# A gate matrix stored by group of 96 tokens, and one-hot tiles with the row number innermost, in a two-layer decoder trunk

## The chip, the core and the metric

The kernel runs on one core of one Trainium2 chip. The core has five engines that work through their own instruction lists in order: TensorE (PE, with its weight loads listed apart as PEld), VectorE (DVE), ScalarE (ACT), GpSimd (POOL) and SyncE (SP). ACT, SP and POOL also issue DMA transfers, and 16 DMA engines carry them out. The metric is the device time of one execution in microseconds (us), lower is better.

## What is computed

The reference is a decoder trunk of two layers on 512 tokens of width 1024. Each layer has a mixer (a gated linear recurrence and a state-space branch), which the change does not touch, and then a PEER block: 8 heads choose 16 of 16384 single-neuron experts for each token.

```python
s1_v, s1_i = lax.top_k(s[:, :, 0, :], PEER_TOPK)
s2_v, s2_i = lax.top_k(s[:, :, 1, :], PEER_TOPK)
cand_v = (s1_v[..., :, None] + s2_v[..., None, :])...
top_v, top_j = lax.top_k(cand_v, PEER_TOPK)
idx = jnp.take_along_axis(cand_i, top_j, axis=-1)
gate = jax.nn.softmax(top_v, axis=-1)
act = jax.nn.gelu(einsum('thkd,td->thk', u_tab[idx], hb))
out = einsum('thk,thkd->td', gate * act, v_tab[idx])
```

An expert number is 128 times a first index plus a second index, so the 16384 experts are a square of 128 by 128.

## The kernel before

For the first 384 tokens (TD) the kernel does not gather. It computes the activation of all 16384 experts and multiplies it by a gate matrix that is zero wherever an expert was not chosen. For the last 128 tokens it gathers the chosen rows. A layer's PEER block has these parts:

- **Scores and select.** `select(tb)` finds, for a block of 128 tokens, the 128 chosen expert numbers of each token and their gates. Most of it is DVE work, among it 128 small operations that write the tile `jk` (L875).
- **Build.** `build(tb, sel, g8)` makes the gate matrix for 4 tokens. There are 96 builds in a layer. For each token it needs a one-hot matrix of the first indices (`P_`, L920), one of the second indices (`Q_`, tile `Qo`, L922) and the second one times the gate, split into two f16 parts (`Q`, L926, twice). A tile has 128 slots (partitions), 128 row numbers and 4 tokens, 512 f16 elements in a partition. DVE makes all four tiles by TENSOR_TENSOR, comparing `io4`, which holds the row numbers, with the token's slot numbers, which are broadcast along the row numbers. PE multiplies `P_` by the two `Q` tiles for each token (L932 and L933, 8 matmuls of 128x128 in a build, into PSUM tile `pa`, two buffers), and ACT copies the result to `stg` (L934). `stg` has one buffer and holds 96 tokens (SG), 24 builds. When it is full, ACT's queue issues four DMAs (L938), each for 32 of the 128 first indices, to the DRAM matrix `sW`. `sW` is ordered by first index, second index, token, with 384 tokens in a row.
- **U matmuls.** `dense_U` multiplies 128 blocks of the expert table by the activations. A block is loaded (`raw`, 512 KB, issued by SP), split by ACT into `whi` (L113) and by DVE into `wlo` (L115), goes through 24 matmuls on PE (L131 to L133, PSUM tile `mm`, three buffers), then through a GELU on ACT into `uo` (L797, two buffers) and to DRAM (`sA`, L798).
- **Gather steps.** `gather_steps` fetches 128 rows of the U table and then 128 rows of the V table, each 512 KB, with DMAs that POOL issues; DVE does a product with each U row (L967) and adds each V row to `gacc` (L978).
- **V matmuls.** For each of the 128 first indices, `gated` loads one row block of `sA` and one of `sW` (tiles `A` and `W`, issued by SP), multiplies them on DVE (L1023), splits the product (`gh` on ACT, `gl` on DVE), and `vmm` does 24 matmuls (L1036 to L1038). The accumulators take all PSUM banks, and a gate block is complete only when all four groups of 96 tokens are in DRAM, so no V matmul starts before the last group has landed.

The code writes builds, U matmuls and gather steps side by side. A list scheduler puts the instructions in each engine's order when the program is built. In layer 0 the work of preparing layer 1's state-space branch (`next_layer`) is added to the V part; in layer 1 it is not.

In this document the **build stage** is the stretch from a layer's first `P_` to the last copy into `stg`, the **gap** is from there to the first V matmul, and the **V stage** follows it.

Of the kernel before, what the change touches and what calls it, by code (L numbers as in the profile page):

```python
# [4 lines left out]
F32 = mybir.dt.float32  # L5
F32R = mybir.dt.float32r
F16 = mybir.dt.float16
# [4 lines left out]
OP = mybir.AluOpType  # L12
# [7 lines left out]
L = 2  # L20
# [7 lines left out]
HPN = 500  # L28
TD = 384
SG = 96  # L30
GB = 3
HALVES = (slice(0, T // 2), slice(T // 2, T))
EPS = 1e-6
# [7 lines left out]
def trunk(tc, a, dbg=None, layers=L, n_i2=128):  # L41
    nc = tc.nc
    V, S, G, TE = nc.vector, nc.scalar, nc.gpsimd, nc.tensor
    uid = [0]

    def nm(s):
        uid[0] += 1
        return f"{s}{uid[0]}"
# [3 lines left out]
    cst = ctx.enter_context(tc.tile_pool(name="cst", bufs=1))  # L52
# [3 lines left out]
    drp = ctx.enter_context(tc.tile_pool(name="drp", bufs=1, space=DRAM))  # L56
    PB = {"mm": 3, "pa": 2, "pb": 2, "pc": 1}

    def ptile(shape, tag):
        return psp.tile(shape, F32, tag=tag, name=nm(tag), bufs=PB[tag])  # L60
# [11 lines left out]
    it = ctmp.tile([128, 128], I32, name="it")  # L72
# [3 lines left out]
    V.memset(ones, 1.0)  # L76
    iof = cst.tile([128, 128], F32, name="iof")
    V.tensor_copy(iof, it)
    io4 = cst.tile([128, 128, 4], F16, name="io4")
    V.tensor_copy(io4, it[:, :, None].to_broadcast([128, 128, 4]))  # L80
    masks = cst.tile([128, 6, 128], U8, name="masks")
    xo = ctmp.tile([128, 128], I32, name="xo")
    V.tensor_tensor(xo, ip, it, op=OP.bitwise_xor)
# [705 lines left out]


    sA = [drp.tile([128, 128, TD], F32, name=f"sA{l}") for l in range(L)]
    sW = [drp.tile([128, 128, TD], F32, name=f"sW{l}") for l in range(L)]

    def dense_U(l, i, h, pool):
        ps = dense(a["u"][l, i], h, n=TD)
# [22 lines left out]
    def peer(l, h, rows, gp):  # L818
# [85 lines left out]
        stg = {}  # L904

        def build(tb, sel, g8):
            st, gh = sel
            NT = 4
            c = slice(NT * g8, NT * g8 + NT)
            t0 = 128 * tb + NT * g8  # L910
            n, o = divmod(t0, SG)
            if o == 0:
                stg[0] = rp.tile([128, 128, SG], F32, tag="stg", name=nm("stg"), bufs=1)
            sh = [128, 128, NT]

            def row(t):
                return t[:, None, :].to_broadcast(sh)

            P_ = rp.tile(sh, F16, tag="P", name=nm("P"))
            V.tensor_tensor(P_, io4, row(st[:, 0, c]), op=OP.is_equal)  # L920
            Q_ = rp.tile(sh, F16, tag="Qo", name=nm("Qo"))
            V.tensor_tensor(Q_, io4, row(st[:, 1, c]), op=OP.is_equal)  # L922
            Qs = []
            for i in range(2):
                q = rp.tile(sh, F16, tag=f"Q{i}", name=nm("Q"))
                V.tensor_tensor(q, Q_, row(gh[:, i, c]), op=OP.mult)  # L926
                Qs.append(q)
            for b in range(NT // 4):
                ps = ptile([128, 4, 128], "pa")
                for k in range(4):  # L930
                    t = 4 * b + k
                    TE.matmul(ps[:, k], P_[:, :, t], Qs[0][:, :, t], start=True, stop=False)  # L932
                    TE.matmul(ps[:, k], P_[:, :, t], Qs[1][:, :, t], start=False, stop=True)  # L933
                S.activation(stg[0][:, :, o + 4 * b:o + 4 * b + 4], ps[:].rearrange("p t i -> p i t"), AF.Copy,  # L934
                             scale=1.0 / GATE)
            if o + NT == SG:
                for q in range(0, 128, 32):
                    nc.scalar.dma_start(sW[l][q:q + 32, :, SG * n:SG * n + SG].rearrange("i p t -> p i t"),  # L938
                                        stg[0][:, q:q + 32])


        def gather_ids(fx):
# [12 lines left out]
        def gather(tab, ids, s_):  # L955
            g = gp.tile([128, D], F32, tag="gr", name=nm("gr"), bufs=GB)
            G.indirect_dma_start(out=g[:], out_offset=None, in_=tab,  # L957
                                 in_offset=bass.IndirectOffsetOnAxis(ap=ids[:, s_:s_ + 1], axis=0))
            return g
# [43 lines left out]
        for tb in range(NB - 1):  # L1003
            sel = select(tb)
            for g8 in range(32):
                build(tb, sel, g8)
                if g8 % 2:
                    more(1)
                    gsteps(1)
# [7 lines left out]
        vctx = ExitStack()  # L1017
        vp = vctx.enter_context(tc.tile_pool(name=f"vp{l}", bufs=2))

        def gated(i, A):  # L1020
            W = vp.tile([128, TD], F32, tag="W", name=nm("W"), bufs=3)
            nc.sync.dma_start(W, sW[l][i])
            V.tensor_tensor(A, A, W, op=OP.mult)  # L1023
            gh = vp.tile([128, TD], F32R, tag="gh", name=nm("gh"), bufs=4)
            S.activation(gh, A, AF.Copy)  # L1025
            gl = vp.tile([128, TD], F32R, tag="gl", name=nm("gl"), bufs=4)
            V.tensor_tensor(gl, A, gh[:].bitcast(F32), op=OP.subtract)  # L1027
            return gh, gl
# [19 lines left out]
        def spilled(i):  # L1048
            w = wv(i)
            A = vp.tile([128, TD], F32, tag="A", name=nm("A"), bufs=3)  # L1050
            nc.sync.dma_start(A, sA[l][i])
            return w, gated(i, A)
# [35 lines left out]
    for k in ("adab", "n1g", "n2g", "glub"):  # L1088
        sh = a[k].shape
# [12 lines left out]
    for j in range(J):  # L1102
        m = cst.tile([128, 2], F32, name=nm("m"))
        for k in range(2):
            t = ad0.tile([128, D], F32, tag="ada", name=nm("ada"))
# [35 lines left out]
    for l in range(layers):  # L1141
        h = norm_mod(gain1[l], shift1[l], ssq, G if l == 0 else None)
        mixer(l, h)
        dump(f"x1_{l}", xT)
        gain2 = mod_gain(l, 4, vec["n2g"][:, l, :])
        gp = tc.alloc_tile_pool(name=f"gp{l}", bufs=1, side="right")
        rows = gp.tile([128, D], F32, name=f"rows{l}")
        h2 = norm_mod_halves(col(gain2), col(mod[l], 24), rows)
        ssq = None

        ssq = peer(l, h2, rows, gp)
        gp.release()
        dump(f"x2_{l}", xT)
# [61 lines left out]
```

## Time and profile before

| | |
|---|---|
| time, median of 3 runs | 4118.07 us (4112.74 to 4119.02) |
| time of the profiled execution | 4119.27 us |
| its span (first to last instruction) | 4117.5 us |
| TensorE clock granted, mean over the span | 0.956 of full speed |
| PE / DVE / ACT / POOL busy | 3748.1 / 3272.4 / 1576.5 / 897.0 us |
| share of the chain that ended last: PE / DVE / DMA / ACT's queue | 67% / 14% / 7% / 4% |
| layer 0: build stage, gap, V stage | 930.6 to 1457.8, to 1497.0, to 2116 us |
| layer 1: build stage, gap, V stage | 2997.9 to 3523.3, to 3560.8, to 4093.5 us |

Busy time is the time in which an engine has at least one instruction under way; instructions that overlap are not counted twice. The chain that ended last is followed back from the end of the program, at each step to what released the instruction. "ACTq" is ACT's instruction queue, here while it issues DMAs. The rows that are read further down come in numbered groups.

### The profile page before, as it was taken

The numbers are of one execution on the slowest core, as the hardware profiler recorded it, in microseconds if no ns is written. First come the engines' busy times: TensorE is split into PE (matmuls) and PEld (weight loads), VectorE is DVE, ScalarE is ACT, GpSimd is POOL, SyncE is SP. The second block draws the span as 40 slices with busy tenths as digits, with TensorE's granted clock in tenths as the row PEclk, the third lists the DMA queues.
The fourth block names the chain that finished last, engine by engine and source line by source line (L and its number), as shares of the span: only waits on it lengthen the run. The fifth ranks groups of instructions, "written<-read, shape, count | busy, mean of one in ns | idle before, by whom it ended". The sixth has DMA issues, their size and how long they took to land.

```text
span 4117.5 us, 63112 instructions
## 1 busy us (share of the span) xinstructions
PE 3748.1 (91%) x21878; PEld 3506.5 (85%) x21878; DVE 3272.4 (79%) x9052; ACT 1576.5 (38%) x2510; POOL 897.0 (22%) x1139
## 2 busy tenths in 40 slices
PE   6999999999698856989999999999996988699998
PEld 5888878999597856889998888789996878699998
DVE  6998778999797769998757777779997976688874
ACT  3554534434233322344443445333342333233332
POOL 7443100033132235532000000000331213222210
PEclk9999999999798978999999999999998989899999
DMA  5222462498788899999843334624987788999994
GB/s 193 72 68 73 156 195 85 150 333 306 215 285 262 281 295 329 362 355 327 280 155 117 123 116 161 211 89 143 322 305 238 262 261 283 306 348 344 347 311 142
DMA packets 463889, 947.60 MB, mean 230 GB/s; under 512 B 169728, under 2 KB 288576, under 8 KB 461520
## 3 DMA queue, kind: packets, MB, share of 16 engines
q1 hardware_dynamic: 220448, 572.75, 41.0%
q0 software_dynamic: 73952, 268.56, 18.9%
q10 hardware_dynamic: 169168, 102.25, 8.4%
q8 instruction: 172, 2.82, 0.3%
q14 instruction: 149, 1.22, 0.1%
HBM read 814.44 MB, written 128.97 MB: 229 GB/s over the span
## 4 chain that ended last, share of the span: by engine, by line
PE 67%; DVE 14%; DMA 7%; ACTq 4%; issue 4%; ACT 2%; POOL 2%; SPq 0%; DVEq 0%; POOLq 0%
PE mm L131 11%; PE mm L132 11%; PE mm L133 11%; ACTq L938 3%; DVE jk L875 3%; PE mm L1037 3%; PE mm L1038 3%; PE mm L1036 3%; DVE wlo L115 3%; DMA gr<-ur,idi 2%; DMA gr<-v,idi 2%; PE pa L933 2%; PE pa L932 2%; PE pa L1037 2%; PE pb L1037 2%
## 5 line engine op out<-in xcount | busy, mean ns | idle before, releaser
L131 PE MATMUL mm<-ahi,whi 128*128 128x384 f32 (+1 forms) x3360 | 1225.2, 366 | 88.3 <-ACT uo L797 82.2
L113 ACT ACTIVATE whi<-raw 128x1024 fp32r<-128x1024 f32 x688 | 727.9, 1059 | 1350.6 <-PE mm L132 755.5
L132 PE MATMUL mm<-alo,whi 128*128 128x384 f32 (+1 forms) x3360 | 1221.6, 364 | 15.7 <-DVE alo L122 15.7
L133 PE MATMUL mm<-ahi,wlo 128*128 128x384 f32 (+1 forms) x3360 | 1221.5, 365 | 9.2 <-DVE wlo L115 9.0
L115 DVE TENSOR_TENSOR wlo<-raw,whi 128x1024 fp32r<-128x1024 f32 x688 | 840.9, 1223 | 378.8 <-ACT whi L113 377.8
L131 PEld LDWEIGHTS mm<-ahi,whi 128*128 128x128 f32 x3360 | 643.4, 192 | 141.1 <-ACT uo L797 86.0
L132 PEld LDWEIGHTS mm<-alo,whi 128*128 128x128 f32 x3360 | 642.4, 191 | 65.5 <-DVE alo L122 17.3
L133 PEld LDWEIGHTS mm<-ahi,wlo 128*128 128x128 f32 x3360 | 641.7, 191 | 62.4 <-DVE wlo L115 13.8
L957 POOL DMA_INDIRECT gr<-ur,idi x256 | 278.7, 1089 | 1498.4 <-DVE jk L875 567.4
L957 POOL DMA_INDIRECT gr<-v,idi x256 | 374.9, 1465 | 737.6 <-DVE gacc L978 645.0
L978 DVE SCALAR_TENSOR_TENSOR gacc<-gr,gate,gacc 128x1024 f32<-128x1024 f32 x254 | 324.6, 1278 | 38.1 <-DMA gr<-v,idi 38.0
L1036 PE MATMUL mm<-gh,whi 128*128 128x384 f32 x768 | 217.8, 341 | 141.4 <-ACT gh L1025 55.5
L967 DVE SCALAR_TENSOR_TENSOR gr<-gr,rows 128x1024 f32<-128x1024 f32 x256 | 311.1, 1217 | 17.6 <-DMA gr<-ur,idi 17.1
L1037 PE MATMUL mm<-gl,whi 128*128 128x384 f32 x768 | 260.8, 340 | 5.7 <-DVE gl L1027 5.3
L1036 PEld LDWEIGHTS mm<-gh,whi 128*128 128x128 f32 x768 | 141.8, 191 | 145.1 <-ACT gh L1025 97.7
L1038 PE MATMUL mm<-gh,wlo 128*128 128x384 f32 x768 | 254.2, 337 | 0.3 <-DVE wlo L115 0.3
L1025 ACT ACTIVATE gh<-A 128x384 fp32r<-128x384 f32 x256 | 132.7, 520 | 284.9 <-DVE A L1023 280.8
L932 PE MATMUL pa<-Q,P 128*128 128x128 f16 x768 | 197.3, 296 | 25.1 <-DVE P L920 15.9
L875 DVE SCALAR_TENSOR_TENSOR jk<-iof,tf,ci 128x50 f32<-128x50 f32 x1024 | 220.1, 267 | 0.0
L934 ACT ACTIVATE stg<-pa 128x512 f32<-128x512 f32 x192 | 114.2, 598 | 241.8 <-PE pa L933 239.5
L933 PE MATMUL pa<-Q,P 128*128 128x128 f16 x768 | 189.0, 296 | 0.2
L1036 PE MATMUL pb<-gh,whi 128*128 128x384 f32 x512 | 173.3, 338 | 0.0
(410 smaller groups left out, 6541.8 us busy)
## 6 DMA issues: line engine op xcount, KB each, us to landing
raw<-u SPq DMA_DIRECT2D x256, 512.0 KB, 5.1
raw<-v SPq DMA_DIRECT2D x256, 512.0 KB, 5.5
raw<-win SPq DMA_DIRECT2D x112, 512.0 KB, 3.7
ada<-ada SPq DMA_DIRECT2D x96, 512.0 KB, 4.8
sA<-uo ACTq DMA_DIRECT2D x256, 192.0 KB, 4.5
sW<-stg ACTq DMA_DIRECT2D x32, 1536.0 KB, 15.2
A<-sA SPq DMA_DIRECT2D x256, 192.0 KB, 5.2
W<-sW SPq DMA_DIRECT2D x256, 192.0 KB, 5.3
```

The source lines that it names most:

```text
L113: S.activation(hi, raw, AF.Copy)
L115: V.tensor_tensor(lo, raw, hi[:].bitcast(F32), op=OP.subtract)
L131: TE.matmul(ps, hi[:, w], ah, start=(j == 0), stop=False)
L132: TE.matmul(ps, hi[:, w], al, start=False, stop=False)
L133: TE.matmul(ps, lo[:, w], ah, start=False, stop=(j == J - 1))
L875: V.scalar_tensor_tensor(jk, iof[:, 0:NCAND], tf[:, hh, k:k + 1], ci[:, hh], op0=OP.is_equal, op1=OP.mult, accum_out=code[:, hh, k:k + 1])
L957: G.indirect_dma_start(out=g[:], out_offset=None, in_=tab, in_offset=bass.IndirectOffsetOnAxis(ap=ids[:, s_:s_ + 1], axis=0))
L967: V.scalar_tensor_tensor(g, g, 1.0, rows, op0=OP.mult, op1=OP.mult, accum_out=dot[:, s_:s_ + 1])
L978: V.scalar_tensor_tensor(acc_, g, gate[:, s_:s_ + 1], acc_, op0=OP.mult, op1=OP.add)
L1036: TE.matmul(ps, w[0][:, c], g[0], start=first, stop=False)
L1037: TE.matmul(ps, w[0][:, c], g[1], start=False, stop=False)
L1038: TE.matmul(ps, w[1][:, c], g[0], start=False, stop=last)
```

## The change

The gate matrix `sW` is now ordered by group of 96 tokens, second index, first index, token in the group. A partition of `stg` holds, for one second index, the first indices and their 96 tokens, so a store of 32 first indices writes 12288 contiguous bytes for a partition; before it wrote 32 pieces of 384 bytes. The loads of the V part now take two first indices at a time (WG), for all four groups: 512 pieces of 768 bytes, where two loads of 128 pieces of 1536 bytes stood. The tile `W` has two buffers of two blocks, before three of one.

The one-hot tiles turn from (row number, token) to (token, row number). `io4` and the four tiles lie in the new order; the slot and gate operands are now broadcast along the innermost dimension, so that in a run of 128 elements they give the same value again and again. Before, they were broadcast along the middle one, and their innermost run was the 4 tokens. PE reads a token's 128 columns from neighbouring places, before from every fourth.

```diff
+WG = 2
...
-    io4 = cst.tile([128, 128, 4], F16, name="io4")
-    V.tensor_copy(io4, it[:, :, None].to_broadcast([128, 128, 4]))
+    io4 = cst.tile([128, 4, 128], F16, name="io4")
+    V.tensor_copy(io4, it[:, None, :].to_broadcast([128, 4, 128]))
...
-    sW = [drp.tile([128, 128, TD], F32, name=f"sW{l}") for l in range(L)]
+    sW = [drp.tile([TD // SG, 128, 128, SG], F32, name=f"sW{l}") for l in range(L)]
...
-            sh = [128, 128, NT]
+            sh = [128, NT, 128]
...
-                return t[:, None, :].to_broadcast(sh)
+                return t[:, :, None].to_broadcast(sh)
...
-                    TE.matmul(ps[:, k], P_[:, :, t], Qs[0][:, :, t], start=True, stop=False)
-                    TE.matmul(ps[:, k], P_[:, :, t], Qs[1][:, :, t], start=False, stop=True)
+                    TE.matmul(ps[:, k], P_[:, t], Qs[0][:, t], start=True, stop=False)
+                    TE.matmul(ps[:, k], P_[:, t], Qs[1][:, t], start=False, stop=True)
...
-                    nc.scalar.dma_start(sW[l][q:q + 32, :, SG * n:SG * n + SG].rearrange("i p t -> p i t"),
-                                        stg[0][:, q:q + 32])
+                    nc.scalar.dma_start(sW[l][n, :, q:q + 32], stg[0][:, q:q + 32])
...
-            W = vp.tile([128, TD], F32, tag="W", name=nm("W"), bufs=3)
-            nc.sync.dma_start(W, sW[l][i])
-            V.tensor_tensor(A, A, W, op=OP.mult)
+            k = i % WG
+            if k == 0:
+                wt[0] = vp.tile([128, TD // SG, WG, SG], F32, tag="W", name=nm("W"), bufs=2)
+                nc.sync.dma_start(wt[0], sW[l][:, :, i:i + WG].rearrange("n p i t -> p n i t"))
+            Av = A[:].rearrange("p (n t) -> p n t", t=SG)
+            V.tensor_tensor(Av, Av, wt[0][:, :, k], op=OP.mult)
```

The scheduler puts the instructions in another order. Between a layer's first and 49th `P_`, DVE makes 50 `wlo` tiles before the change and 80 after it; between the first and last one, 20 additions to `gacc` before and 55 after it in layer 0 (18 and 54 in layer 1). The products with U rows (95) and the `jk` operations (250) in that stretch are as many as before.

The first place is DVE in layer 0 in the third group of 24 builds. Qo, P and Q are the one-hot tiles, gr and gacc belong to gather steps, wlo to a U matmul block. Before:

```order
L922 TENSOR_TENSOR Qo_11646<-io_83,slot_11420 128x512
L920 TENSOR_TENSOR P_11589<-io_83,slot_11420 128x512
L926 TENSOR_TENSOR Q_11593<-Qo_11591,gh_11422 128x512
L926 TENSOR_TENSOR Q_11595<-Qo_11591,gh_11422 128x512
L115 TENSOR_TENSOR wlo_14978<-raw_14974,whi_14976 128x1024
L920 TENSOR_TENSOR P_11644<-io_83,slot_11420 128x512
L967 SCALAR_TENSOR_TENSOR gr_15415,dot_8446<-gr_15415,rows_6308 128x1024
```

The same place on DVE after the change:

```order
L921 TENSOR_TENSOR P_11589<-io_83,slot_11420 128x512
L978 SCALAR_TENSOR_TENSOR gacc_6543<-gr_17504,gate_8444,gacc_6543 128x1024
L927 TENSOR_TENSOR Q_11575<-Qo_11573,gh_11422 128x512
L927 TENSOR_TENSOR Q_11577<-Qo_11573,gh_11422 128x512
L927 TENSOR_TENSOR Q_11593<-Qo_11591,gh_11422 128x512
L927 TENSOR_TENSOR Q_11595<-Qo_11591,gh_11422 128x512
L978 SCALAR_TENSOR_TENSOR gacc_6543<-gr_17546,gate_8444,gacc_6543 128x1024
```

The U blocks are gone from this stretch (they stand ahead of it now), and additions to `gacc` stand in the place of products with U rows.

The second place is ACT in layer 0 around the third store of `stg`; whi and uo belong to U blocks, dot to the gather steps. Before:

```order
L938 DMA sW_121<-stg_10488 128x32x96 x4
L970 ACTIVATE dot_8446<-dot_8446 128x32
L113 ACTIVATE whi_15124<-raw_15122 128x1024
L797 ACTIVATE uo_15042<-mm_15017 128x384
L798 DMA sA_119<-uo_15042 128x384
```

After the change:

```order
L935 ACTIVATE stg_10488<-pa_11670 128x128x4
L939 DMA sW_121<-stg_10488 128x3072 x4
L935 ACTIVATE stg_11721<-pa_11730 128x128x4
L935 ACTIVATE stg_11721<-pa_11748 128x128x4
L935 ACTIVATE stg_11721<-pa_11803 128x128x4
```

Behind the store stands at once the first copy into the next `stg`, which needs the buffer that the store is reading.

## Rows read from the trace of the kernel before

**Rows 1.** The page: the chain that ended last, by line.

```profile
PE mm L131 11%; PE mm L132 11%; PE mm L133 11%; ACTq L938 3%; DVE jk L875 3%; PE mm L1037 3%; PE mm L1038 3%; PE mm L1036 3%; DVE wlo L115 3%; DMA gr<-ur,idi 2%; DMA gr<-v,idi 2%; PE pa L933 2%; PE pa L932 2%; PE pa L1037 2%; PE pb L1037 2%
```

**Rows 2.** Stages: length, busy PE, PEld, DVE, ACT, POOL, clock, DMA share, GB/s.

```profile
930.60:1457.80 527.20, 455.73 (x2772) 431.32 (x2771) 423.52 (x1274) 177.52 (x270) 133.86 (x117) 0.92 0.83 266
1457.80:1497.00 39.20, 0.00 (x0) 0.00 (x0) 11.35 (x18) 4.11 (x6) 6.23 (x6) 0.50 1.00 268
1497.00:2116.00 619.00, 549.48 (x3071) 541.65 (x3071) 525.40 (x1139) 238.85 (x356) 193.59 (x116) 0.95 0.90 321
2997.90:3523.30 525.40, 454.95 (x2772) 431.48 (x2771) 422.38 (x1273) 178.44 (x271) 136.40 (x116) 0.92 0.83 267
3523.30:3560.80 37.50, 0.00 (x0) 0.00 (x0) 9.90 (x11) 3.50 (x5) 7.03 (x6) 0.50 1.02 284
3560.80:4093.50 532.70, 532.68 (x3071) 532.68 (x3071) 399.87 (x487) 196.63 (x254) 106.98 (x101) 1.00 0.89 314
```

**Rows 3.** ACT around the second store, in order of time: start, length, idle before.

```profile
1229.58 22.70 ACTq L938 DMA_DIRECT2D sW<-stg  x4
1252.38 1.06 ACT L113 ACTIVATE whi<-raw 128x1024 fp32r<-128x1024 f32 x1 [22.83 <-issue]
```

**Rows 4.** DVE's waits in layer 0's build stage: total us, times, longest.

```profile
DVE wlo L115 <- ACT whi L113: 59.9, 24, 23.1
DVE gate L971 <- ACT dot L970: 20.2, 1, 20.2
DVE P L920 <- PE pa L933: 10.5, 14, 1.5
DVE Q L926 <- PE pa L932: 8.3, 6, 3.2
```

**Rows 5.** DVE instructions by form over the run: busy us, mean ns, idle before.

```profile
L926 DVE TENSOR_TENSOR Q<-Qo,gh 128x512 f16<-128x512 f16 x384 | 149.2, 421 | 19.1 <-PE pa L932 19.0
L920 DVE TENSOR_TENSOR P<-io,slot 128x512 f16<-128x512 f16 x192 | 80.2, 420 | 21.6 <-PE pa L933 20.8
L922 DVE TENSOR_TENSOR Qo<-io,slot 128x512 f16<-128x512 f16 x192 | 78.1, 418 | 0.0
...
L757 DVE TENSOR_TENSOR ya<-ya,sg 128x512 f32<-128x512 f32 x16 | 11.0, 685 | 0.0
...
L115 DVE TENSOR_TENSOR wlo<-raw,whi 128x1024 fp32r<-128x1024 f32 x688 | 840.9, 1223 | 378.8 <-ACT whi L113 377.8
...
L978 DVE SCALAR_TENSOR_TENSOR gacc<-gr,gate,gacc 128x1024 f32<-128x1024 f32 x254 | 324.6, 1278 | 38.1 <-DMA gr<-v,idi 38.0
```

**Rows 6.** PE in order of time, f16 build matmuls and f32 U matmuls.

```profile
986.51 0.30 PE L933 MATMUL pa<-Q,P 128*128 128x128 f16 x1
986.63 0.30 PE L932 MATMUL pa<-Q,P 128*128 128x128 f16 x1
...
988.17 0.33 PE L131 MATMUL mm<-ahi,whi 128*128 128x384 f32 x1
...
988.52 0.33 PE L133 MATMUL mm<-ahi,wlo 128*128 128x384 f32 x1
```

**Rows 7.** DMA queues from 1230 to 1262 us (packets, MB, share of 16 engines).

```profile
q10 hardware_dynamic: 16645, 6.57, 80.2%
...
q1 hardware_dynamic: 288, 1.05, 9.3%
```

**Rows 8.** DMA issues on their queues: ns min/median/max, first and last start.

```profile
L938 ACTq DMA_DIRECT2D sW<-stg x32: 377/5910/10732, 1068.0 to 3537.6; - x32
...
L810 SPq DMA_DIRECT2D s5t<-pk x8: 319/373/589, 1688.8 to 2022.8; - x8
```

**Rows 9.** Page, DMA issues: KB each, us to landing.

```profile
s5t<-pk SPq DMA_DIRECT2D x8, 2176.0 KB, 9.4
```

**Rows 10.** The end of layer 0's gap on ACT, and the V matmuls' first start.

```profile
1488.96 2.95 ACT L113 ACTIVATE whi<-raw 128x1024 fp32r<-128x1024 f32 x3 [30.56 <-DMA sW<-stg]
...
L1036 PE MATMUL mm<-gh,whi x384: 333/334/689, 1497.0 to 2110.6; 128*128 128x384 f32 x192
```

More of the change, by code (lines that the diff above doesn't have):

```diff
@@ L1018, in peer @@
         vp = vctx.enter_context(tc.tile_pool(name=f"vp{l}", bufs=2))
+        wt = [None]
         def gated(i, A):
-            W = vp.tile([128, TD], F32, tag="W", name=nm("W"), bufs=3)
-            nc.sync.dma_start(W, sW[l][i])
-            V.tensor_tensor(A, A, W, op=OP.mult)
+            k = i % WG
[4 more added lines that the diff above has]
+            V.tensor_tensor(Av, Av, wt[0][:, :, k], op=OP.mult)
             gh = vp.tile([128, TD], F32R, tag="gh", name=nm("gh"), bufs=4)
```

## The prediction

> **What bounds the kernel now.** I read the chain that ended last first, then the windows by stage, then DVE's waits and the single durations. The chain lies on PE for the most part, but one line of it is no work at all: ACT's queue stands 3% of the span at L938, the store of the gate matrix [rows 1]. That is the first thing to explain. The windows then say which engine is near its limit in each stage [rows 2]. In the last stage, layer 1's V stage, PE is busy in 532.68 of 532.70 us, so nothing but PE counts there. Layer 0's V stage takes 619.0 us for the same PE instructions; PE is idle for 70 us of it, DVE is busy for 525 and the DMA engines for 90%. In the two build stages (527.2 and 525.4 us) PE is busy for 456 and 455 us and DVE for 423.5 and 422.4.
>
> DVE's 104 idle us in layer 0's build stage are the key. The four DMAs of one store hold ACT's queue for 22.7 us, and ACT's next instruction, the `whi` of a U block, comes 22.83 us late [rows 3]. DVE waits for ACT in the same moments: single waits of 23.1 us for `whi` and 20.2 us for `dot` [rows 4]. Three such stores lie inside a build stage. What remains of DVE's waiting for PE, for free one-hot tiles, is 10.5 and 8.3 us [rows 4], 18.8 us in all. So outside the stores PE and DVE are both nearly full, and whatever lengthens DVE's work in the build stage lengthens the stage once the stores no longer hold ACT.
>
> **The change part by part.**
>
> *The store's pieces.* A store was 4 DMAs of 4096 pieces of 384 bytes; it becomes 4 of 128 pieces of 12288 bytes. The queue time was 5.9 us for a median DMA of it. The store of `pk`, 17408 bytes in each of 128 partitions, is issued in 0.37 us [rows 8], and that is the nearest row in shape: 4 x 0.37 = 1.5 us instead of 22.7. The data time by the queue's rows: 80.2% of 16 engines over 32 us is 411 us for 16645 packets, 24.7 ns each, nearly all of 384 bytes; 9.3% is 47.6 us for 1.05 MB, 256 packets of 4096 bytes, 186 ns each [rows 7]. A line through both gives an estimate of 542 ns for 12288 bytes, so 512 x 542 / 16 = 17 us for a store; by the landing time of `pk`, 2176 KB in 9.4 us [rows 9], the 6144 KB would take 27 us. The bounds are 17 and 27; I take 19, nearer the price of a packet, because ACT's queue has little else in it. Inside the build stage the gain shows only as DVE's waits for ACT going away, which the sum below does. In the gap it shows directly. The gap of layer 0 was 39.2 us: the last store was landed when ACT went on at 1489.0, and the first V matmul began 8.0 us later [rows 10]. Now it is 1.5 + 19 + 8 = 28.5 us, 11 us less; in layer 1, from 37.5 us [rows 2], 9 us less.
>
> *The one-hot tiles on DVE.* This is the largest term. Four operations a build, 384 a layer, take 418 to 421 ns for 512 f16 elements. With f32 operands of the same size a TENSOR_TENSOR takes 685 ns, and one of 1024 elements 1223 [rows 5]. So a step of f32 costs (1223 - 685) / 512 = 1.05 ns an element, 147 ns are fixed, and f16 runs at (420 - 147) / 512 = 0.53 ns: two elements in a step. No row shows f16 with one operand that repeats along the innermost dimension, which is what the slot and gate operands now do. The bounds are 420 (pairs are still formed) and 685 ns (one element at a time). Before, each operand had 4 different neighbours in its innermost run; now one operand has no neighbour to pair with, only the same place again. I take 685, the row of one element a step, and keep 420 as a rival. The price is 265 ns x 384 = 101.8 us of DVE a layer. The Trainium skill (Vector Engine (DVE) Microarchitecture Reference, section 5.1 Performance modes) speaks against the change here: it asks a step of plus or minus 1 of every source for the mode of two 16-bit values, and reports one element read 16 times as either source of a two-source 2-byte operation at one per cycle on trn2. By that rule the 265 ns stand; no run here shows it yet.
>
> *The matmuls' columns.* A build's f16 matmuls start 0.12 us apart, and two f32 ones 0.35 us, 0.175 each [rows 6]. PE now reads neighbouring columns. The bounds are no gain and half of the 0.12 us; 768 matmuls a layer would give 0 to 46 us of PE. I take none: in the sum DVE sets the build stage.
>
> *The order.* The scheduler puts 80 of the stage's 82 U blocks ahead of the 49th build, before the change 50. The second half of the builds has DVE alone to feed it, with 35 more additions to `gacc` in layer 0 and 36 in layer 1, 1.278 us each [rows 5]: 44.7 and 46.0 us of DVE come into the build stages and leave the V stages.
>
> *The build stages.* DVE's work is 423.5 + 101.8 + 44.7 = 570.0 us in layer 0 and 422.4 + 101.8 + 46.0 = 570.2 in layer 1. PE's work (456 and 455 us) fits under it, ACT's and POOL's too [rows 2]. I leave 18.8 us for waits in each, those for PE [rows 4], and drop those for ACT: 588.8 against 527.2 is +61.6 us, 589.0 against 525.4 is +63.6.
>
> *The V stages.* Layer 1's is PE's alone, so the `gacc` work that left it gives nothing: 0. In layer 0's, DVE and the DMA engines were nearly full, so the 44.7 us give back something between 0 and 44.7; PE's 70 idle us there are only partly due to them, and I take 20. The W loads are now of 768 bytes: by the line above 41 ns, against 75 for 1536, so 256 x 41 / 16 = 0.66 us a block where it was 0.60. That is 8 us of DMA time a layer, hidden in layer 1 by PE, with 11% of the DMA time free [rows 2]; uncovered it would cost 8 us a layer. SP issues 64 such loads a layer instead of 128; a load of 512 pieces lies between 0.37 us and an eighth of 5.9 us [rows 8], and SP is ahead of PE there. The product on DVE works on f32 in both cases: nothing.
>
> *The sum.* 61.6 - 11 - 20 + 63.6 - 9 + 0 = +85 us on the profiled execution's 4119.27 us, which is 1.2 us above the median of the runs: **4203 us**.
>
> **The rivals.**
>
> *Pairs are still formed* (the one-hot operations stay at 420 ns; this ends at faster or no change). The build stage then has two parts. In the first PE is the limit: 82 U blocks x 24 x 0.175 us plus 50 builds x 8 x 0.12 us is 392 us. In the second DVE: 46 builds x 4 x 0.42 plus 54 additions x 1.278 is 146. Together 538 us: +11 and +13. With the gaps and V stages as above the sum is 11 - 11 - 20 + 13 - 9 = -16 us, 4103; waits of up to 22 us in each stage bring it to 4147. For it speaks only that no row shows the slow form. It decides below some 575 ns an operation: there 423.5 + 45 + 18.8 + 0.384 x 155 = 547 us a stage, +20 us twice, which the gaps and layer 0's V stage pay for.
>
> *The store becomes a wait for its buffer.* `stg` has one buffer. After the third store ACT's order has a copy into the next `stg` at once, so ACT stands there until the store is read, 17 to 27 us, where it stood in the queue before. DVE can run ahead by two PSUM buffers and two sets of tiles, 4 builds x 4 x 0.685 = 11 us, and a few additions. If each of the six inner stores costs DVE 8 us, the time is 4203 + 48 = 4251; without that cover, 6 x 19, 4317. Nearest to it: if a store's issue were slow by its bytes and not its pieces, so that ACT is held as before; the 0.37 us of `pk` speak against it.
>
> *DVE runs without any wait, and layer 0's V stage takes back all 44.7 us*: 85 - 2 x 18.8 - 24.7 = +23 us, 4142. DVE's waits behind PE were never zero, which speaks against it.
>
> **How the numbers follow.** The forecast, with the build stages between 575 and 610 us: 0.57, some 4165 to 4245. Pairs still formed: 0.17 (0.08 faster, 0.05 the same, 0.04 slower). The buffer's wait: 0.15. No waits at all: 0.11. About 0.2% is what a measurement of this kernel can tell from no change, 8 us. So faster 0.08, same 0.05, slower 0.87. The range goes from 4112 to 4265: it leaves out the faster end of the first rival and the far end of the second.
>
> **What would show it.** The one-hot operations at about 685 ns, or at 420. L938 at about 0.4 us a DMA. DVE busy for some 570 us of a build stage of about 590, and PE mostly idle in its second half, where the granted clock may fall. A gap under 30 us. Layer 1's V stage still at 533 us. The prediction is wrong if the one-hot operations are below 575 ns, if ACT stands long before the copies into `stg`, or if layer 1's V stage grows, which would be the 768-byte loads.

## The result, and the profile after

The changed kernel takes 4220.47 us (median of 4 runs, 4216.12 to 4221.75); the kernel before, timed beside it, 4118.55 (4112.74 to 4119.83). The ratio is 1.0248, with a 95% interval from 1.0231 to 1.0266: slower by 102 us, where 85 were forecast. The profiled execution of after has a span of 4218.9 us. As elsewhere here, a build stage runs from the first `P_` to the last copy into `stg`; the gap and the V stage follow it.

The page of after: first the busy time of the engines, then the chain by line, which answers to [rows 1], then one group of instructions (busy us, mean ns of one, idle before), which answers to the first line of [rows 5].

```profile
PE 3697.2 (88%) x21878; PEld 3455.5 (82%) x21878; DVE 3469.7 (82%) x9052; ACT 1565.0 (37%) x2510; POOL 993.7 (24%) x1139
...
PE mm L134 10%; PE mm L132 10%; PE mm L133 10%; DMA sW<-stg 3%; DVE wlo L116 3%; PE mm L1042 3%; PE mm L1043 3%; PE mm L1041 3%; DVE jk L876 2%; DMA gr<-ur,idi 2%; DVE Q L927 2%; DMA gr<-v,idi 2%; DVE gacc L978 2%; PE pa L1043 2%; PE pb L1043 2%
...
L927 DVE TENSOR_TENSOR Q<-Qo,gh 128x512 f16<-128x512 f16 x384 | 244.6, 680 | 25.3 <-PE pa L933 25.3
```

ACT's queue, 3% of the chain before, has left it. In its place stand the store's data and, new, DVE's one-hot line L927. The one-hot operations went from 421 to 680 ns.

The windows by stage of after, with the columns of [rows 2] (length; busy PE, PEld, DVE, ACT, POOL; clock, DMA share, GB/s): build stage, gap, V stage of layer 0, then the same of layer 1. The V stages are cut where the transposes of `gacc` begin.

```profile
932.60:1528.80 596.20, 433.43 (x2772) 406.88 (x2770) 562.28 (x1309) 175.68 (x270) 237.07 (x152) 0.82 0.78 267
1528.80:1559.80 31.00, 0.02 (x1) 0.02 (x1) 12.76 (x19) 4.14 (x6) 8.29 (x8) 0.50 0.95 355
1559.80:2141.60 581.80, 530.50 (x2999) 526.25 (x3000) 478.72 (x1096) 233.55 (x352) 104.25 (x80) 0.96 0.88 305
3034.20:3630.70 596.50, 430.79 (x2772) 403.90 (x2771) 560.79 (x1308) 175.76 (x271) 239.25 (x151) 0.82 0.78 266
3630.70:3660.00 29.30, 0.01 (x1) 0.01 (x1) 12.30 (x13) 4.12 (x6) 8.19 (x7) 0.50 0.98 378
3660.00:4183.30 523.30, 523.30 (x3004) 523.30 (x3005) 352.73 (x444) 190.02 (x252) 83.81 (x64) 0.99 0.83 283
```

The V stages of before, cut at the same place:

```profile
1497.00:2104.80 607.80, 538.28 (x3000) 530.45 (x3001) 518.94 (x1132) 235.58 (x352) 193.59 (x116) 0.95 0.90 323
3560.80:4082.80 522.00, 521.98 (x3004) 521.98 (x3005) 395.08 (x481) 194.64 (x252) 106.98 (x101) 1.00 0.91 320
```

Against [rows 2] the build stages grew by 69.0 and 71.1 us and both gaps shrank by 8.2. Layer 0's V stage shrank by 26.0, layer 1's grew by 1.3. That is 99 of the 102 us. DVE is now the engine that is nearly full in a build stage (562 of 596 us; before, 423 of 527). Its instructions there went from 1274 to 1309: the 35 additions that the order had announced. They stand in the second half, where PE has little to do. Windows of 50 us, one before that half and two in it:

```profile
1280.00:1330.00 50.00, 43.39 (x279) 41.80 (x278) 47.95 (x129) 13.14 (x21) 16.11 (x12) 0.98 0.97 363
1330.00:1380.00 50.00, 14.76 (x106) 10.17 (x106) 48.43 (x148) 9.10 (x16) 11.43 (x10) 0.50 0.43 135
1480.00:1530.00 50.00, 15.44 (x112) 11.32 (x112) 49.97 (x69) 8.36 (x14) 41.36 (x14) 0.50 0.47 142
```

In the last two windows PE is busy for 15 of 50 us, DVE for 48 and more, and the granted clock is at 0.50, the lower of TensorE's two levels. In the two windows of 50 us between them, which are not shown, DVE is busy for 43 and 41 us: there it waits 10.8 us for gathered rows and 4.6 us for PE.

The waits of DVE and ACT in layer 0's build stage after (total us, times, longest), which answer to [rows 3] and [rows 4]:

```profile
ACT stg L935 <- DMA sW<-stg: 54.7, 3, 22.5
PE pa L933 <- ACT stg L935: 34.2, 3, 16.6
DVE Q L927 <- PE pa L933: 12.1, 5, 4.7
DVE gacc L978 <- DMA gr<-v,idi: 10.8, 8, 4.2
DVE P L921 <- PE pa L934: 5.5, 6, 2.0
DVE gr L967 <- DMA gr<-ur,idi: 3.4, 6, 1.6
DVE wlo L116 <- ACT whi L114: 1.9, 2, 1.0
```

DVE waits 1.9 us for `whi` where it waited 59.9, but 33.7 us in all, not 18.8. ACT now stands three times before a copy into `stg`, until the store before it has been read.

### The profile page after: what moved, and what is told of

Read it like the earlier page. It is cut to its first block, busy times and chain, and to the rows that moved or that the text cites. A ratio compares the mean times of both kernels' runs of the same rounds, so it can differ in the third digit from the quotient of the medians.

```text
span 4218.9 us, 62845 instructions
## 1 busy us (share of the span) xinstructions
PE 3697.2 (88%) x21878; PEld 3455.5 (82%) x21878; DVE 3469.7 (82%) x9052; ACT 1565.0 (37%) x2510; POOL 993.7 (24%) x1139
## 3 DMA queue, kind: packets, MB, share of 16 engines
q0 software_dynamic: 73952, 268.56, 18.8%
## 4 chain that ended last, share of the span: by engine, by line
PE 61%; DVE 19%; DMA 11%; issue 4%; POOL 3%; ACT 2%; ACTq 0%; SPq 0%; DVEq 0%; POOLq 0%
PE mm L134 10%; PE mm L132 10%; PE mm L133 10%; DMA sW<-stg 3%; DVE wlo L116 3%; PE mm L1042 3%; PE mm L1043 3%; PE mm L1041 3%; DVE jk L876 2%; DMA gr<-ur,idi 2%; DVE Q L927 2%; DMA gr<-v,idi 2%; DVE gacc L978 2%; PE pa L1043 2%; PE pb L1043 2%
## 5 line engine op out<-in xcount | busy, mean ns | idle before, releaser
L134 PEld LDWEIGHTS mm<-ahi,wlo 128*128 128x128 f32 x3360 | 635.9, 189 | 65.3 <-DVE wlo L116 16.4
L957 POOL DMA_INDIRECT gr<-ur,idi x256 | 317.2, 1239 | 1360.1 <-DVE jk L876 648.8
L957 POOL DMA_INDIRECT gr<-v,idi x256 | 433.0, 1691 | 590.3 <-DVE gacc L978 452.9
L933 PE MATMUL pa<-Q,P 128*128 128x128 f16 x768 | 154.3, 267 | 263.2 <-DVE Q L927 189.9
L967 DVE SCALAR_TENSOR_TENSOR gr<-gr,rows 128x1024 f32<-128x1024 f32 x256 | 310.1, 1213 | 23.6 <-DMA gr<-ur,idi 23.4
L1041 PE MATMUL mm<-gh,whi 128*128 128x384 f32 x768 | 235.2, 340 | 107.6 <-DMA raw<-v 60.3
L933 PEld LDWEIGHTS <-P 128*128 128x128 f16 x768 | 87.9, 115 | 280.1 <-DVE Q L927 220.9
L927 DVE TENSOR_TENSOR Q<-Qo,gh 128x512 f16<-128x512 f16 x384 | 244.6, 680 | 25.3 <-PE pa L933 25.3
```

Of the source, the lines that this page charges most:

```text
L134: TE.matmul(ps, lo[:, w], ah, start=False, stop=(j == J - 1))
L957: G.indirect_dma_start(out=g[:], out_offset=None, in_=tab, in_offset=bass.IndirectOffsetOnAxis(ap=ids[:, s_:s_ + 1], axis=0))
L1041: TE.matmul(ps, w[0][:, c], g[0], start=first, stop=False)
```

## The experiments

In what follows each kernel's time stands with its ratio to the kernel before, timed beside it (medians of 4118.4 to 4119.0 us), and the 95% interval.

**The two halves of the change apart.** First the new layout of `sW` and the paired loads of `W`, with the tiles as they were:

```diff
-    io4 = cst.tile([128, 4, 128], F16, name="io4")
+    io4 = cst.tile([128, 128, 4], F16, name="io4")
...
-            sh = [128, NT, 128]
+            sh = [128, 128, NT]
...
-                    TE.matmul(ps[:, k], P_[:, t], Qs[0][:, t], start=True, stop=False)
+                    TE.matmul(ps[:, k], P_[:, :, t], Qs[0][:, :, t], start=True, stop=False)
```

> The gate matrix lies by group of 96 tokens and is loaded two blocks at a time, as after the change; the one-hot tiles stay as they were before. If the slower one-hot operations are the cause of the loss (theory): they run at 420 ns, ACT's queue is held for under 2 us by a store, the build stages shrink to 475 to 495 us, the gaps to about 30, and the time is 3990 to 4040 us. If the new store and loads are the cause (the store's landing becomes a wait for the one buffer of stg, 768-byte loads slow the V stage): 4180 us or more.

It took 4037.6 us (0.9806, 0.9790 to 0.9822). Then the new tiles alone, with the old `sW` and one load for each `W`:

```diff
-    sW = [drp.tile([TD // SG, 128, 128, SG], F32, name=f"sW{l}") for l in range(L)]
+    sW = [drp.tile([128, 128, TD], F32, name=f"sW{l}") for l in range(L)]
...
-                    nc.scalar.dma_start(sW[l][n, :, q:q + 32], stg[0][:, q:q + 32])
+                    nc.scalar.dma_start(sW[l][q:q + 32, :, SG * n:SG * n + SG].rearrange("i p t -> p i t"),
+                                        stg[0][:, q:q + 32])
```

> The one-hot tiles have the row number innermost, as after the change; the gate matrix in DRAM stays as it was before. Theory: one-hot operations at 680 ns, ACT held 22 us by each store, build stages of 580 to 600 us, gaps of 38, time 4215 to 4260 us. If the store and loads were the cause of the loss, this kernel runs at the time of the kernel before, 4118 us.

It took 4263.69 us (1.0354, 1.0337 to 1.0371), a little above what was expected. Layer 0's build stage, with the store alone and with the tiles alone:

```profile
929.90:1427.10 497.20, 451.45 (x2772) 425.36 (x2771) 436.29 (x1286) 177.86 (x270) 159.83 (x129) 0.93 0.85 295
```

```profile
931.40:1534.30 602.90, 430.97 (x2772) 404.03 (x2771) 536.02 (x1288) 174.88 (x270) 225.75 (x131) 0.83 0.76 246
```

So the change is two opposite ones: the store brings 81 us, the tiles cost 145. Their sum is +64, and 102 were measured, so the two don't add up. The build stage says why. DVE's idle time is its length less its busy time: 103.7 us before [rows 2], 60.9 with the store alone, 66.9 with the tiles alone, 33.9 with both. By itself the store saves 42.8 idle us and brings 12 more additions than before (1286 against 1274 instructions), and 30 us are left. On top of the tiles it still saves 33 idle us, but with both changes there are 35 more additions than before in the stage, where the tiles alone had 14 more (1288 against 1274 instructions). These 21 x 1.278 = 27 us use up nearly all of the 33.

**Is it the repeated place or the orientation?** The changed kernel again, but with each value of slot and gate stored twice side by side. The innermost run of the repeated operand is then two neighbours, and the row number stays innermost. Three small integer tiles share the buffers of others, to make room.

```diff
-            st = rp.tile([128, 2, 128], F16, tag="slot", name=nm("slot"))
-            S.activation(st, pt[:, 0:2], AF.Copy)
+            st = rp.tile([128, 2, 128, 2], F16, tag="slot", name=nm("slot"))
+            for k in range(2):
+                S.activation(st[:, :, :, k], pt[:, 0:2], AF.Copy)
...
-                return t[:, :, None].to_broadcast(sh)
+                return t[:, :, None, :].to_broadcast([128, NT, 64, 2])
```

> The changed kernel, but each slot number and gate lies twice, side by side, so that the broadcast operand's innermost run is two equal neighbours instead of one place read again; everything else of the new layout stays (three small tiles of select share buffers to make room). If the repeated place is what costs the second element of a step (theory): one-hot operations at 420 ns, build stages of 470 to 500 us, time 3985 to 4040 us. If it is the new order of the tiles (row number innermost) as such, they stay at 680 ns and the time at 4200 to 4240 us.

It took 4022.2 us (0.9763, 0.9747 to 0.9779). Its one-hot groups:

```profile
L931 DVE TENSOR_TENSOR Q<-Qo,gh 128x512 f16<-128x512 f16 x384 | 146.7, 424 | 25.6 <-PE pa L937 25.6
L925 DVE TENSOR_TENSOR P<-io,slot 128x512 f16<-128x512 f16 x192 | 78.5, 424 | 0.3 <-PE pa L938 0.3
```

From 680 back to 424 ns, with the same elements in the same places of `P_` and `Q_`: the cost lies in the operand that repeats one place, not in the new order of the tiles. The Trainium skill (Vector Engine (DVE) Microarchitecture Reference, section 5.1 Performance modes) asks a step of plus or minus 1 and more than one element in the innermost dimension of every source; 680 ns without it and 424 with two neighbours agree with that.

**What the additions cost.** The changed kernel with `gacc` allocated in the V stage's pool, so that no addition can stand in a build stage:

```diff
-        gacc = gp.tile([128, D], F32, name=f"gacc{l}")
...
+        gacc = gaccs[0] = vp.tile([128, D], F32, name=f"gacc{l}", tag="gacc", bufs=1)
```

> The changed kernel, but the tile gacc is taken only when the V stage begins, so that none of the 55 additions to it lies in a build stage. One-hot operations stay at 680 ns. If DVE's sum of work sets the build stage (theory): each build stage loses 55 x 1.28 = 70 us, layer 0's V stage gains some 45 of them back, layer 1's at most 5, and the time is 4120 to 4150 us. If the additions only fill time in which DVE would wait anyway, the time stays at 4220 us or grows.

It took 4120.28 us (1.0006, 0.9993 to 1.0019), no different from the kernel before, with the one-hot operations at 689 ns. Its two build stages:

```profile
930.30:1452.10 521.80, 434.11 (x2772) 402.78 (x2771) 494.02 (x1252) 175.84 (x270) 124.33 (x96) 0.87 0.71 250
3011.00:3532.80 521.80, 434.00 (x2772) 403.86 (x2770) 494.38 (x1252) 175.30 (x271) 127.04 (x96) 0.86 0.71 250
```

They are 74.4 and 74.7 us shorter than after's. Gap and V stage together grew by 53 us in layer 0 (612.8 to 665.9), but not in layer 1 (552.6 to 549.0), where PE sets the time and DVE had 170 idle us. The same edit on the kernel before:

> The kernel before, with gacc taken only when the V stage begins, so that its 20 additions leave each build stage. Theory (a layer's build stage is set by DVE's sum where ACT does not hold it, and layer 1's V stage has room on DVE): up to 20 x 1.28 = 26 us less in each build stage, some 15 back in layer 0's V stage, 4085 to 4115 us. If the additions stand in the moments in which DVE waits for ACT's store anyway: 4115 to 4130 us.

It took 4117.63 us (0.9996, 0.9985 to 1.0006): the theory's gain did not come, the other expectation held. Build stage of layer 0, and DVE's largest waits in it:

```profile
931.50:1449.00 517.50, 451.12 (x2758) 427.84 (x2757) 399.10 (x1252) 177.14 (x269) 105.55 (x96) 0.92 0.78 251
```

```profile
DVE wlo L115 <- ACT whi L113: 67.3, 25, 23.6
DVE gate L970 <- ACT dot L969: 19.1, 1, 19.1
```

DVE's busy time fell by 24.4 us, but the stage by 9.7 only: the waits for ACT, which the stores hold, stayed and grew (67.3 for 59.9). Layer 1's build stage is 13.8 us shorter. Layer 0's gap and V stage together took 14.8 us of this back (661.8 for 647.0), and another 7 us went outside these stages. The additions cost little there because DVE had time to wait in; where DVE sets the stage they cost 100 us.

**Without either cost.** Pairs and held additions together, with the store's new layout:

> Slot numbers and gates twice side by side, and gacc taken when the V stage begins: the 43 additions leave the build stages of the kernel with pairs. Theory: DVE has some 400 us in a build stage then and PE, at 0.06 us for an f16 matmul, some 400 to 420; the stage falls from 495 to 445 to 465 us, layer 0's V stage takes some 30 us back, the time is 3955 to 4000 us. If the wait for the one buffer of stg sets the stage: 4000 to 4025 us.

It took 3962.36 us (0.9625, 0.9609 to 0.9641). To see what PE's neighbouring columns are worth, the new store and held additions with the old tiles:

> The new store and loads, the old one-hot tiles, and gacc taken when the V stage begins. Theory: PE, whose f16 matmuls read every fourth column here and take 0.12 us each, has 451 us of work in a build stage, so the stage falls only from 497 to some 475 us; the time is 4000 to 4035 us and stays 30 us or more above the kernel with pairs and held additions. If the columns' distance does not matter for the time: within 10 us of that one.

It took 4009.93 us (0.9736, 0.9720 to 0.9753). DVE's one-hot operations have the same price in both. Of the 48 us between them, 22.5 and 19.1 lie in the build stages. Build stage of layer 0, with the new tiles in pairs and with the old ones:

```profile
930.90:1378.00 447.10, 412.34 (x2740) 389.88 (x2738) 389.64 (x1222) 173.97 (x269) 116.27 (x95) 0.95 0.81 287
```

```profile
933.30:1402.90 469.60, 449.14 (x2773) 427.87 (x2771) 397.09 (x1252) 178.18 (x270) 106.94 (x96) 0.96 0.79 277
```

PE, the engine that is nearly full in both, is busy for 37 us less, DVE for 7. Not all of this is the columns: the scheduler put 33 matmuls of the U blocks fewer into the stage with pairs (2740 against 2773 instructions of PE), at 0.175 us each [rows 6] an estimate of 6 us. The timelines show where the rest comes from, first the new tiles in pairs, then the old ones (start us, length):

```profile
1104.22 0.22 PE L938 MATMUL pa<-Q,P 128*128 128x128 f16 x1
1104.28 0.22 PE L937 MATMUL pa<-Q,P 128*128 128x128 f16 x1
1104.34 0.22 PE L938 MATMUL pa<-Q,P 128*128 128x128 f16 x1
```

```profile
1228.52 0.29 PE L934 MATMUL pa<-Q,P 128*128 128x128 f16 x1
1228.63 0.30 PE L933 MATMUL pa<-Q,P 128*128 128x128 f16 x1
1228.75 0.30 PE L934 MATMUL pa<-Q,P 128*128 128x128 f16 x1
```

A build matmul starts 0.06 us after the one before it where neighbouring columns are read, and 0.12 us where every fourth is. No run turns only one of a matmul's two operands, so which of them sets the distance stays open.

**The one buffer of `stg`.** In the kernel with pairs and held additions, PE still waits 24.3 us in a build stage behind copies into `stg`. Half the group (48 tokens) in two buffers:

```diff
-SG = 96
+SG = 48
...
-                stg[0] = rp.tile([128, 128, SG], F32, tag="stg", name=nm("stg"), bufs=1)
+                stg[0] = rp.tile([128, 128, SG], F32, tag="stg", name=nm("stg"), bufs=2)
```

> As the kernel with pairs and held additions, but the gate matrix goes out in groups of 48 tokens from two buffers of stg, so that no copy waits for a store; a partition's store piece has 6144 bytes, a load's 384. Theory: each of three waits of 8 to 18 us in a build stage goes, 10 to 35 us a stage, and the shorter pieces of the loads cost up to 15 us in layer 0's V stage: 3930 to 3985 us, 10 to 40 us less than the kernel with one buffer. If other work covers those waits: the same time, or longer by the loads.

It took 4005.85 us (0.9730, 0.9710 to 0.9750), a miss. The build stages are shorter, by 13.1 and 15.5 us (434.0 for 447.1 in layer 0), but layer 1's V stage takes 589.5 us instead of 524.3. The gap ahead of it is not in these numbers; the expectations of the next two runs count it in, as 608 and 550 us. Layer 1's V stage with pairs and held additions, and then with two buffers:

```profile
3396.70:3921.00 524.30, 523.21 (x3000) 522.71 (x3001) 425.35 (x503) 196.16 (x250) 167.00 (x123) 0.99 0.97 343
```

```profile
3380.60:3970.10 589.50, 537.17 (x2999) 525.80 (x3000) 421.31 (x500) 191.17 (x250) 148.73 (x123) 0.98 0.92 304
```

With two rows a load, the pieces of a `W` load are now 48 x 2 x 4 = 384 bytes. With four rows they are 768 again (and `gh` and `gl` of the V stage have two buffers, not four, to make room):

```diff
-WG = 2
+WG = 4
```

> As the kernel with two buffers of stg, but four blocks to a load, so that a load's piece is 768 bytes again (the tiles gh and gl have two buffers instead of four, to make room). If the 384-byte pieces made layer 1's V stage 608 us long: it falls back to some 550, the build stages stay at 430 to 435, and the time is 3920 to 3960 us. If the smaller groups or the second buffer did it: 3990 us or more.

It took 3945.21 us (0.9577, 0.9561 to 0.9593), the fastest of all, 173 us below the kernel before; layer 1's V stage took 524.4 us:

```profile
3388.90:3913.30 524.40, 523.76 (x2999) 523.25 (x3000) 421.73 (x501) 192.35 (x249) 141.56 (x122) 0.99 0.94 341
```

To separate the pieces from the buffers, the kernel with one `stg` of 96 tokens and one row a load (384 bytes, three buffers of `W`):

```diff
-WG = 2
+WG = 1
```

> As the kernel with pairs and held additions, but one block to a load, so that a load has 512 pieces of 384 bytes (three buffers of one block, as before the change). If pieces of 384 bytes slow the V stages: layer 1's grows from 550 to some 600 us and layer 0's by 10 to 20, 4010 to 4040 us. If the V stage does not feel the piece's size: 3955 to 3970 us.

It took 4053.86 us (0.9847, 0.9828 to 0.9867), 92 us more than with two rows a load: the pieces matter, by more than was expected. Layer 1's V stage took 592.6 us. Its middle, 3500 to 3700 us, with 768-byte pieces and then with 384:

```profile
3500.00:3700.00 200.00, 200.00 (x1156) 200.00 (x1155) 161.26 (x190) 75.08 (x95) 65.66 (x49) 1.00 0.97 345
```

```profile
3500.00:3700.00 200.00, 182.84 (x1037) 178.99 (x1036) 143.67 (x171) 64.67 (x85) 42.89 (x42) 1.00 0.94 306
```

The DMA engines are busy nearly all the time in both (0.97 and 0.94), but move 345 GB/s in the one and 306 in the other; PE, full in the first, is idle for 17 of 200 us in the second. This kernel also has twice as many loads and holds three blocks of `W` ahead instead of four. That these alone do not slow the stage can be read from the kernel before, which had as many loads and the same three buffers, but pieces of 1536 bytes: 200 us from the middle of its layer 1's V stage show PE full and 346 GB/s.

```profile
3600.00:3800.00 200.00, 200.00 (x1155) 200.00 (x1155) 161.28 (x191) 75.07 (x96) 51.45 (x50) 1.00 0.98 346
```

The Trainium skill (DMA: Bandwidth & Descriptors, Specifications) puts the smallest transfer for the line rate at 512 bytes; 768 and 384 lie on either side of that, and the two kernels agree with it.

## Why the prediction was right, step by step

*The one-hot tiles on DVE.* 685 ns were taken, from the f32 row, and 680 measured (690 and 689 in the second and fourth experiments, which have the same tiles). That is 99.8 us a layer instead of 101.8. The first rival, pairs still formed, is out; the third experiment shows the reason given to be the cause.

*The order and the build stages.* 35 additions came in layer 0, as counted. DVE's busy time was put at 570.0 and 570.2 us and came to 562.3 and 560.8, in part since its other operations, too, were some nanoseconds shorter than before (`wlo` 1213 for 1221 in this stage). **The mis-sized term is DVE's waits**: 18.8 us were left for them, the waits for PE in [rows 4], and 33.9 and 35.7 came (length less busy time). The rows of after name them: for PE 12.1 + 5.5 = 17.6 us, near to what was taken, and, not foreseen, 10.8 and 3.4 us for gathered rows (`gr`) that had not landed. The 10.8 us come with the additions that were moved forward: before the change none of those in layer 0's build stage waited, as their row in that stage shows (count, busy us, mean ns, idle before).

```profile
L978 DVE SCALAR_TENSOR_TENSOR gacc<-gr,gate,gacc 128x1024 f32<-128x1024 f32 x21 | 26.8, 1278 | 0.0
```

The 3.4 us are for the products with U rows and do not come with the additions, since 5.5 of that kind were seen with them held back. The net error of the build stages is 7.4 us in layer 0 (596.2 for 588.8) and 7.5 in layer 1.

*The store's pieces.* ACT no longer holds up DVE, as said. The issue is dearer than `pk`'s 0.37 us: 0.96 median, where it was 5.91 [rows 8]:

```profile
L939 ACTq DMA_DIRECT2D sW<-stg x32: 326/964/1743, 1106.4 to 3633.2; - x32
```

The gaps were put at 28.5 us in both layers and came to 31.0 and 29.3. In layer 0 the issue of the last store took 3.61 us, where 1.5 were taken. From there to ACT's next instruction, which waits for the store, 18.7 us passed, where 19 were taken for the data. The row of that instruction after the change, which answers to the first of [rows 10]:

```profile
1551.73 2.95 ACT L114 ACTIVATE whi<-raw 128x1024 fp32r<-128x1024 f32 x3 [22.31 <-DMA sW<-stg]
```

*The rival of `stg`'s one buffer* is partly true: ACT waits 54.7 us for three stores and PE 34.2 behind it. It does not become the bound in the changed kernel, since DVE waits for PE for no more than 17.6 us. How much of those it causes was not tried on the changed kernel itself; in the kernel with pairs and held additions two smaller buffers made the build stages 13.1 and 15.5 us shorter.

*The matmuls' columns.* No gain was taken, with 46 us a layer as the other end. The matmuls do start at half the distance, so the upper end was the right one for PE alone; in the changed kernel this stays hidden, as PE's busy time (433 us) lies far below DVE's. It comes out where DVE is shorter: 48 us in both layers together between the sixth and seventh experiments, some of it the scheduler's different order.

*The V stages.* Layer 0's gave 26 us for a forecast of 20, layer 1's changed by 1.3 for a forecast of 0. The 768-byte loads stayed hidden under PE there: DMA share 0.83.

*The sum.* Build stages +140.1 (forecast +125.2), gaps -16.4 (-20), V stages -24.7 (-20): +99, with some 3 us elsewhere, for +85. The 15 us too few in the build stages are most of the difference: DVE's waits came out 32 us longer there than was taken, its work 17 us shorter. That these two errors partly cancel is luck.

## What to carry to other kernels

Before turning a layout for one engine's reads, follow what the innermost step becomes for each of the others: here it halved the distance between PE's matmuls and took from DVE its two elements a step, and storing the repeated value twice gave both. Where a stage's bound moves to another engine, count what the scheduler puts into that stage of that engine's work which could wait: some 20 additions in each build stage could be taken out for no gain in time while DVE waited anyway, and taking out some 55 from each gained 100 us in all once it did not. Size a DRAM layout by the reader's pieces as much as by the writer's.

## What the runs showed of the hardware that was not expected

- A 128-column f16 matmul of the build started 0.06 us after the one before it with neighbouring columns and 0.12 us with a step of four, both at a granted clock of 1.0. With neighbouring columns at the lower level (0.50) the distance was 0.11 us, as these rows of the changed kernel show:

```profile
1411.53 0.31 PE L934 MATMUL pa<-Q,P 128*128 128x128 f16 x1
1411.64 0.31 PE L933 MATMUL pa<-Q,P 128*128 128x128 f16 x1
```

- Loads of the same bytes in pieces of 384 instead of 768 bytes lengthened layer 1's V stage from 524 to 593 us. In the middle of it the DMA engines' share did not rise (0.97, then 0.94), but they moved 306 instead of 345 GB/s.
- Twelve-kilobyte pieces still cost ACT's queue time: the four DMAs of the last store before layer 0's gap held it for 3.61 us, against 22.7 us for four of 4096 pieces [rows 3]. The row of after (start us, length):

```profile
1529.44 3.61 ACTq L939 DMA_DIRECT2D sW<-stg  x4
```
